# One queue for the first block's two pieces, and the sample's output products behind block 1, whose last half is accumulated in two banks

## The chip, the cores and the metric

The kernel runs on one core of a Trainium2 chip. The metric is the device time of one execution in microseconds (us), and the profile is one execution taken by the hardware profiler. The engines are named as in the profile: PE is TensorE's products, PEld its weight loads, ACT is ScalarE, DVE is VectorE, POOL is GpSimd, SP is SyncE; a q behind a name is the engine's own instruction stream (DMA issues, semaphores).

## The reference

One step of a hybrid encoder layer for two groups that share all weights: a prompt of 256 frames and a sample of 32 frames of a running stream, 288 rows in all, width 1024. One input projection feeds an mLSTM branch (4 heads of 256) and a sparse attention branch (8 heads of 128); both are gated, projected and summed to `mixed`. What the change touches is the end of it, and the mLSTM state that the prompt leaves:

```python
C_new = decay * C + einsum('bhs,bshk,bshv->bhkv', w_s, k, v)
n_new = decay * n + einsum('bhs,bshk->bhk', w_s, k)
...
mixed = sigmoid(ga) * (branch_a @ w_out_a) + sigmoid(gb) * (branch_b @ w_out_b)
return layer_norm(DN_ALPHA * x + mixed @ w_o, ln_g, ln_b)
```

The outputs are y for prompt and sample, K, V and indexer keys, and the state C, n and m of both groups.

## The kernel before

The weights are cut into tiles of 1024 x 128, in the order of `tile_order`. Every tile is loaded by SyncE (`load_tile`), split into a high part by ScalarE (`split_hi`, line 130) and a low part by VectorE (`split_lo`, line 137), and multiplied on TensorE three times per 128 rows: high by high, high by low, low by high (`product`). All instructions of an engine run in the order in which the program issues them; the order is written out by hand: the loop of lines 1080 to 1092 goes over the tiles, and `at(slot, fn)` hangs further steps on a tile, which `side()` issues in the middle of that tile's products, in the order in which they were hung there.

**The start.** The first five tiles are loaded in eight blocks of 128 rows, with the matching rows of x (`lead`). Block 0 comes in two pieces: x and the first tile (416 columns), issued by SyncE (line 162), and the other four tiles (512 columns), issued by ScalarE on its own queue (line 163). Blocks 1 to 7 follow on SyncE's queue (line 165). ScalarE casts x to xh (line 170) and the weights to their high part (line 177). Until the first piece is there, TensorE runs 18 products on zeros (`keep_warm`).

**The output weights.** The last eight tiles, `wo`, are 128 rows of w_o each. `natural(t, rows)` multiplies them with `mixed` as the stationary side: rows 0 and 1 are the prompt's two blocks of 128 frames, each in two PSUM banks of 512 columns (yn, line 941); rows 2 is the sample, 32 frames x 1024 columns laid out as 4 groups of 32 partitions x 256 columns, 64 products from the raw weights (line 945). For the first four wo tiles both blocks are multiplied tile by tile; between block 0 and block 1 `side()` issues `k_weighted(h)` for head h (four transposes of its keys into a bank kt, line 687; two halves scaled into kwh by ScalarE, line 691, and the remainder into kwl by VectorE, line 692), and in the fourth tile also `state_prompt(0)`: two times six products of head 0's state (lines 704 to 706), each copied out by ScalarE (line 707), and the output's DMA, issued by ScalarE (line 711). For the last four tiles (`late`) `finish()` goes column half by column half instead: block 0, the sample, block 1; then the states of heads 1 to 3.

**The layer norm.** VectorE forms alpha * x + y in z (`residual`, line 1000), takes bn_stats of each half (line 1002), aggregates them and adds eps (lines 989, 990), GpSimd raises that to -1/2 (line 991), VectorE subtracts the mean and multiplies by g (`centred`, line 1006), and scales and adds b by halves (`scaled`, line 1011), behind which SyncE writes each half of 512 columns (line 1015). The sample goes through the same in 128 x 256 form (lines 1027 to 1042); its statistics are gathered from four groups of 32 partitions and spread back by small copies (lines 1030, 1033, 1035). VectorE's order is: block 0, the sample's statistics, block 0's scaling, first half of block 1, the sample's last two steps, second half of block 1, block 1's scaling.

PSUM has eight banks in two pools: six of `bank()` (tag side), two of tag proj, which the tiles' products and the state products use in turn. Before, kt is of the six.

## Time and profile before

| | us |
|---|---|
| median of 3 runs | 433.31 (433.23 to 433.58) |
| the profiled execution, its own time | 433.03 |
| its span in the profile | 431.3 |
| PE busy, share of the span | 424.0, 98% |
| PEld busy | 412.8, 96% |
| DVE busy | 300.3, 70% |
| ACT busy | 232.5, 54% |
| POOL busy | 23.0, 5% |
| granted TensorE clock, mean | 0.999 |

The span is what the profile shows between the first and the last instruction; the run's own time holds a little before and behind it. Busy shares are averages over stages with different limits. Times within the profile are counted from the span's start. A wait is given in brackets behind the instruction that waited, with what released it.

### The profile page before, as it was taken

How to read it: one execution, taken by the hardware profiler on the slowest of the kernel's cores; microseconds unless marked ns; L12 is line 12 of the kernel's file. 1: busy time of each engine (PE TensorE's matmuls, PEld its weight loads, DVE VectorE, ACT ScalarE, POOL GpSimd, SP SyncE). 2: the span in 40 equal slices, each digit the busy share in tenths (PEclk: the TensorE clock that was granted, in tenths of full speed). 3: DMA queues.
4: the chain of work that ended last, by engine and by line, in shares of the span. 5: the costliest groups of instructions: out<-in, count | busy, mean ns of one | idle time of the engine just before them, and what ended most of it. 6: DMA issues, size and time to landing. Idle time of an engine off the chain costs nothing.

```text
span 431.3 us, 8450 instructions
## 1 busy us (share of the span) xinstructions
PE 424.0 (98%) x3320; PEld 412.8 (96%) x3320; DVE 300.3 (70%) x607; ACT 232.5 (54%) x466; POOL 23.0 (5%) x46
## 2 busy tenths in 40 slices
PE   8999999999999999999999999999999999999994
PEld 7999999999999999999999999999999999998874
DVE  5779888898656665666999887776544465565674
ACT  6776556464475665667695464555343444445402
POOL 2000000021000000000001101101000000000031
PEclk9999999999999999999999999999999999999999
DMA  8996969757845544745554456444665567543014
GB/s 305 337 347 189 280 199 326 240 188 204 293 163 141 154 133 120 256 128 147 147 147 147 106 167 218 134 146 134 181 177 159 158 183 256 155 141 122 26 48 137
DMA packets 23471, 78.05 MB, mean 181 GB/s; under 512 B 2804, under 2 KB 5572, under 8 KB 22632
## 3 DMA queue, kind: packets, MB, share of 16 engines
q1 hardware_dynamic: 22568, 76.21, 57.0%
q10 hardware_dynamic: 864, 1.32, 0.9%
q8 instruction: 26, 0.43, 0.4%
q14 instruction: 13, 0.11, 0.1%
HBM read 71.77 MB, written 7.64 MB: 184 GB/s over the span
## 4 chain that ended last, share of the span: by engine, by line
PE 96%; DVE 1%; DMA 1%; ACT 1%; POOLq 0%; DVEq 0%; issue 0%
PE pj L923 26%; PE pj L922 26%; PE pj L924 25%; PE yn L941 5%; PE pj L960 3%; DMA wst_k<-in_first 1%; PE yn L945 1%; PE apt L592 1%; ACT wh L130 0%; PE al L573 0%; PE ix L416 0%; PE ix L417 0%; PE s L633 0%; PE av L602 0%; PE vt L646 0%; PE kt L687 0%
## 5 line engine op out<-in xcount | busy, mean ns | idle before, releaser
L922 PE MATMUL pj<-xh,wh 128*128 128x288 f32 x704 | 209.8, 298 | 0.1
L923 PE MATMUL pj<-xl,wh 128*128 128x288 f32 x704 | 207.7, 295 | 0.0
L924 PE MATMUL pj<-xh,wl 128*128 128x288 f32 x704 | 207.5, 295 | 0.0
L130 ACT CAST wh<-wst 128x1024 fp32r<-128x1024 f32 x112 | 117.8, 1052 | 128.9 <-PE pj L923 78.1
L137 DVE TENSOR_TENSOR wl<-wst,wh 128x1024 fp32r<-128x1024 f32 x112 | 136.2, 1219 | 29.0 <-ACT wh L130 28.7
L922 PEld LDWEIGHTS pj<-xh,wh 128*128 128x128 f32 x704 | 132.4, 188 | 1.0 <-issue 0.4
L923 PEld LDWEIGHTS pj<-xl,wh 128*128 128x128 f32 x704 | 132.4, 188 | 0.1
L924 PEld LDWEIGHTS pj<-xh,wl 128*128 128x128 f32 x704 | 132.3, 188 | 0.0
L922 PE MATMUL pj<-bbh,wh 128*128 128x288 f32 x64 | 19.1, 298 | 0.0
L923 PE MATMUL pj<-bbl,wh 128*128 128x288 f32 x64 | 19.0, 296 | 0.0
L923 PE MATMUL pj<-bal,wh 128*128 128x288 f32 x64 | 18.9, 295 | 0.0
L924 PE MATMUL pj<-bah,wl 128*128 128x288 f32 x64 | 18.9, 295 | 0.0
L924 PE MATMUL pj<-bbh,wl 128*128 128x288 f32 x64 | 18.8, 294 | 0.0
L922 PE MATMUL pj<-bah,wh 128*128 128x288 f32 x64 | 18.8, 293 | 0.0
L941 PE MATMUL yn<-wh,mxh 128*128 128x512 f32 x32 | 13.0, 407 | 0.0
L941 PE MATMUL yn<-wl,mxh 128*128 128x512 f32 x32 | 12.7, 396 | 0.1
L941 PE MATMUL yn<-wh,mxl 128*128 128x512 f32 x32 | 12.6, 394 | 0.0
L922 PEld LDWEIGHTS pj<-bbh,wh 128*128 128x128 f32 x64 | 12.1, 188 | 0.0
L924 PEld LDWEIGHTS pj<-bbh,wl 128*128 128x128 f32 x64 | 12.0, 188 | 0.0
L922 PEld LDWEIGHTS pj<-bah,wh 128*128 128x128 f32 x64 | 12.0, 188 | 0.0
L923 PEld LDWEIGHTS pj<-bal,wh 128*128 128x128 f32 x64 | 12.0, 188 | 0.0
L924 PEld LDWEIGHTS pj<-bah,wl 128*128 128x128 f32 x64 | 12.0, 188 | 0.0
(494 smaller groups left out, 576.7 us busy)
## 6 DMA issues: line engine op xcount, KB each, us to landing
wst<-in_w SPq DMA_DIRECT2D x112, 512.0 KB, 3.7
wst_k<-in_first SPq DMA_DIRECT2D x7, 464.0 KB, 5.9
rscr<-rrow SPq DMA_DIRECT2D x2, 768.0 KB
out_k<-kbT SPq DMA_DIRECT2D x1, 1152.0 KB
stC<-in_state_C SPq DMA_DIRECT2D x1, 1028.0 KB
out_C_sample<-stC SPq DMA_DIRECT2D x1, 1028.0 KB
bm<-rscr SPq DMA_DIRECT2D x1, 1024.0 KB
ckT<-in_cache_k SPq DMA_DIRECT2D x1, 1024.0 KB
```

The lines of the kernel that those rows point to most:

```text
L130: act.copy(split[t][0], stage[t])
L137: dve.tensor_tensor(wl, stage[t], wh.bitcast(F32), OP.subtract)
L592: pe.transpose(p[:, 128 * i:128 * i + 128], lg[:, c:c + 128], ident)
L922: pe.matmul(p[:, :T], lhsT=wh[:, c], rhs=h[:, k], start=(k == 0), stop=False)
L923: pe.matmul(p[:, :T], lhsT=wh[:, c], rhs=l[:, k], start=False, stop=False)
L924: pe.matmul(p[:, :T], lhsT=wl[:, c], rhs=h[:, k], start=False, stop=(k == KT - 1))
L941: pe.matmul(p, lhsT=x[:, k, r], rhs=w[:, c], start=first and i == 0, stop=last and i == 2)
L945: pe.matmul(p[32 * q:32 * q + 32, 0:256], lhsT=lazy["mxs"][:, k], rhs=stage[t][:, 256 * q:256 * q + 256], start=first, stop=last)
L960: pe.matmul(p[t][:, new], lhsT=w[:, 128 * t:128 * t + 128], rhs=x[:, k, new], start=(k == 0 and w is wh and x is xh), stop=(k == KT - 1 an ...
```

## The change

It does four things. (1) Block 0's second piece is issued by SyncE behind the first, not by ScalarE. (2) The bank kt is taken from the two of tag proj, and in the fourth wo tile `state_prompt(0)` is issued ahead of `k_weighted(3)`. (3) Block 1's second half is accumulated in two banks of 256 columns, in all eight wo tiles, and statistics are taken of 256 columns everywhere (four records per row instead of two). (4) In `finish()` the order is: block 0, block 1, sample, states, on TensorE; block 0, block 1 to its first scaled half, sample, with block 1's second scaled half between the sample's last two steps, on VectorE. Four small copies of the sample's mean go from GpSimd to VectorE.

```diff
     sp.dma_start(lead[0][:, 0:cut], a["first"][:, 0, 0:cut])
-    act.dma_start(lead[0][:, cut:LEAD], a["first"][:, 0, cut:])
+    sp.dma_start(lead[0][:, cut:LEAD], a["first"][:, 0, cut:])
...
-        p = bank(f"kt{h}")
+        p = ps.tile([128, 512], F32, name=f"kt{h}", tag="proj", bufs=2)
...
-    def natural(t, rows, columns=(0, 1)):
+    pieces = (((0, 512), (512, 1024)), ((0, 512), (512, 768), (768, 1024)))
+
+    def natural(t, rows, some=None):
...
-            lazy["yp", rows] = [bank(f"yn{rows}{c}") for c in range(2 if rows < 2 else 1)]
+            lazy["yp", rows] = [bank(f"yn{rows}{c}") for c in range(len(pieces[rows]) if rows < 2 else 1)]
...
-            for c in columns:
-                p = lazy["yp", rows][c]
-                c = slice(512 * c, 512 * c + 512)
+            for j, (c0, c1) in enumerate(pieces[rows]):
+                if some not in (None, j):
+                    continue
+                p = lazy["yp", rows][j][:, :c1 - c0]
+                c = slice(c0, c1)
...
-            dve.bn_stats(bst[:, b, c], z[:, b, half])
+            for c in range(c0, c1, 256):
+                dve.bn_stats(bst[:, b, c // 256], z[:, b, c:c + 256])
...
-        for rows in (0, 2, 1):
-            for c in range(2 if rows < 2 else 1):
-                for t in late if rows < 2 else range(POS["wo", 0], NT):
-                    natural(t, rows, (c,))
-        for c in range(2):
-            residual(0, c)
-        rs = centred(0)
+        for b in range(2):
+            for j in range(len(pieces[b])):
+                for t in late:
+                    natural(t, b, j)
+        for t in range(POS["wo", 0], NT):
+            natural(t, 2)
+        for j in range(len(pieces[0])):
+            residual(0, j)
+        rs = centred(0)
+        for c in range(2):
+            scaled(0, rs, c)
+        for j in range(len(pieces[1])):
+            residual(1, j)
+        rs = centred(1)
+        scaled(1, rs, 0)
...
-        for q in range(4):
-            pool.tensor_copy(nr[32 * q:32 * q + 32, 0:1], mv[r, 0:1])
         for q in range(3):
             pool.tensor_copy(nr[32 * q:32 * q + 32, 1:2], nr[r, 1:2])
-        scaled(0, rs)
-        for c in range(2):
-            put(0, c)
-        residual(1, 0)
+        for q in range(4):
+            dve.tensor_copy(nr[32 * q:32 * q + 32, 0:1], mv[r, 0:1])
         dve.scalar_tensor_tensor(zs, zs, nr[:, 0:1], lazy["gs"], op0=OP.subtract, op1=OP.mult)
+        scaled(1, rs, 1)
         dve.scalar_tensor_tensor(zs, zs, nr[:, 1:2], lazy["bs"], op0=OP.mult, op1=OP.add)
         sp.dma_start(ap_of(o["y"], TP * D, [[256, 4], [D, TS], [1, 256]]), zs)
-        residual(1, 1)
-        rs = centred(1)
-        state_prompt(1)
-        scaled(1, rs)
-        for c in range(2):
-            put(1, c)
-        for h in range(2, AH):
+        for h in range(1, AH):
             state_prompt(h)
...
+    at(POS["wo", 0] + 3, state_prompt, 0)
     for h in range(AH):
         at(POS["wo", 0] + h, k_weighted, h)
-    at(POS["wo", 0] + 3, state_prompt, 0)
```

`scaled(b, rs, c)` now does one half and issues its output.

ScalarE in the fourth wo tile and behind it, before. L130 is the high part of a weight tile (the first row that of the last tile but one, the last row that of the last tile), L691 the scaled keys of head 3, L707 and L711 the state of head 0:

```order
L130 CAST wh_5136<-wst_4938 128x1024
L691 ACTIVATE kwh<-kt_5146,gnat 128x256 x2
L707 COPY oc_all<-c_5156 128x257
L707 COPY oc_all<-c_5164 128x257
L711 DMA out_C_prompt<-oc_all 128x514
L130 CAST wh_5180<-wst_4971 128x1024
```

The same stretch of the change:

```order
L130 CAST wh_5146<-wst_4938 128x1024
L707 COPY oc_all<-c_5157 128x257
L707 COPY oc_all<-c_5165 128x257
L711 DMA out_C_prompt<-oc_all 128x514
L691 ACTIVATE kwh<-kt_5174,gnat 128x256 x2
L130 CAST wh_5193<-wst_4971 128x1024
```

Head 3's two activations, on which VectorE's kwl (line 692) and, in VectorE's order, the low parts of the last two tiles follow, now stand behind the two copies and the DMA issue of head 0's state.

VectorE from block 1's first residual to the end, before. z is the prompt's rows, sq the sample's, yn_5078 and yn_5079 are block 1's banks:

```order
L1000 SCALAR_TENSOR_TENSOR z__5055<-xn,yn_5078 128x512
L1002 BN_STATS bst<-z__5055 128x6
L1040 SCALAR_TENSOR_TENSOR sq<-sq,nr_5281 128x256
L1041 SCALAR_TENSOR_TENSOR sq<-sq,nr_5281 128x256
L1000 SCALAR_TENSOR_TENSOR z__5055<-xn,yn_5079 128x512
L1002 BN_STATS bst<-z__5055 128x6
L989 BN_AGGR mv_5303<-bst 128x2
L990 TENSOR_SCALAR mv_5303<-mv_5303 128x1
L1006 SCALAR_TENSOR_TENSOR z__5055<-z__5055,mv_5303,lngb 128x1024
L1011 SCALAR_TENSOR_TENSOR z__5055<-z__5055,nr_5304,lngb 128x512 x2
```

The end of it in the change, from block 1's last two steps on:

```order
L1012 SCALAR_TENSOR_TENSOR z__5055<-z__5055,mv_5313,lngb 128x1024
L1017 SCALAR_TENSOR_TENSOR z__5055<-z__5055,nr_5314,lngb 128x512
L1038 SCALAR_TENSOR_TENSOR sq<-sq,yn_5257 128x256
L1039 BN_STATS bss<-sq 128x6
L1041 COPY bss<-bss 32x6 x3
L993 BN_AGGR mv_5326<-bss 32x2
L994 TENSOR_SCALAR mv_5326<-mv_5326 32x1
L1046 COPY nr_5327<-mv_5326 32x1 x4
L1047 SCALAR_TENSOR_TENSOR sq<-sq,nr_5327 128x256
L1017 SCALAR_TENSOR_TENSOR z__5055<-z__5055,nr_5314,lngb 128x512
L1049 SCALAR_TENSOR_TENSOR sq<-sq,nr_5327 128x256
```

The whole of the sample's part now stands behind block 1's first scaling, where before it was spread over the steps of both blocks; its last step is VectorE's last.

## Rows read from the trace of the kernel before

**Rows 1.** The page, chain of work that ended last, share of the span by engine.

```profile
PE 96%; DVE 1%; DMA 1%; ACT 1%; POOLq 0%; DVEq 0%; issue 0%
```

**Rows 2.** Timeline of the start: start us, us, engine line op out<-in, [idle before <-releaser].

```profile
0.80 0.41 ACTq L163 DMA_DIRECT2D wst_k<-in_first  x1
...
1.13 3.48 PE L148 MATMUL warm_p<-warm 128*128 128x256 bf16 x18 [1.13 <-DVE warm L143]
...
4.53 0.43 ACT L170 CAST xh<-wst_k 128x288 fp32r<-128x288 f32 x1 [2.00 <-DMA wst_k<-in_first]
...
6.09 0.72 ACT L177 CAST wh_k<-wst_k 128x640 fp32r<-128x640 f32 x1
...
7.27 0.75 PE L960 MATMUL pj<-xh,wh_k 128*128 128x288 f32 x5
```

**Rows 3.** DMA queues, window 2.8 to 3.4: packets, MB, share of 16 engines (q10: ScalarE's).

```profile
q10 hardware_dynamic: 47, 0.10, 49.9%
```

**Rows 4.** Timeline of the fourth wo tile and the late tiles, 402 to 409.

```profile
402.66 0.60 PE L687 MATMUL kt<-cst,kaT 128*128 128x128 f32 x4
...
403.29 0.47 ACT L691 ACTIVATE kwh<-kt,gnat 128x256 fp32r<-128x256 f32 x1 [0.74 <-PE kt L687]
...
404.69 0.64 ACT L707 COPY oc_all<-c 128x257 f32<-128x257 f32 x2
...
404.83 0.48 DVE L692 SCALAR_TENSOR_TENSOR kwl<-kt,gnat,kwh 128x256 fp32r<-128x256 f32 x1 [0.54 <-ACT kwh L691]
...
405.23 1.22 DVE L137 TENSOR_TENSOR wl<-wst,wh 128x1024 fp32r<-128x1024 f32 x1
405.36 0.35 ACTq L711 DMA_DIRECT2D out_C_prompt<-oc_all  x1
...
406.12 1.05 ACT L130 CAST wh<-wst 128x1024 fp32r<-128x1024 f32 x1 [0.78 <-PE yn L941]
...
407.20 1.22 DVE L137 TENSOR_TENSOR wl<-wst,wh 128x1024 fp32r<-128x1024 f32 x1 [0.75 <-ACT wh L130]
...
408.47 0.19 PEld L941 LDWEIGHTS yn<-wl,mxh 128*128 128x128 f32 x1 [0.51 <-DVE wl L137]
```

**Rows 5.** Chain that ended last, from 405 us: start us, us, what.

```profile
411.99 3.59 PE yn L945 x64
415.58 5.80 PE yn L941 x24
```

**Rows 6.** Windows, PE alone, 36 state products: stretch, us, busy (x), clock, DMA share, GB/s.

```profile
421.20:425.48 4.28, 4.28 (x36) 1.00 0.27 92
```

**Rows 7.** Timeline of the layer norm, 412 to 427.

```profile
412.02 0.69 DVE L1000 SCALAR_TENSOR_TENSOR z__5055<-xn,yn 128x512 f32<-128x512 f32 x1 [1.30 <-PE yn L941]
412.75 0.69 DVE L1002 BATCH_NORM_STATS2 bst<-z__5055 128x6 f32<-128x512 f32 x1
...
415.65 0.42 DVE L1027 SCALAR_TENSOR_TENSOR sq<-sq,yn 128x256 f32<-128x256 f32 x1 [0.58 <-PE yn L945]
...
416.10 0.43 DVE L1028 BATCH_NORM_STATS2 bss<-sq 128x6 f32<-128x256 f32 x1
...
416.56 0.52 DVE L1030 COPY bss<-bss 32x6 f32<-32x6 f32 x3
...
417.70 1.06 POOL L991 TENSOR_TENSOR nr<-mv,mhalf 32x1 f32<-32x1 f32 x1 [2.23 <-DVE mv L990]
...
423.09 0.15 DVE L990 TENSOR_SCALAR mv<-mv 128x1 f32<-128x1 f32 x1
...
424.89 1.42 DVE L1011 SCALAR_TENSOR_TENSOR z__5055<-z__5055,nr,lngb 128x512 f32<-128x512 f32 x2 [0.45 <-POOL nr L991]
```

**Rows 8.** Timeline of SyncE's queue: the issue of the sample's output.

```profile
421.32 0.59 SPq L1042 DMA_DIRECT2D out_y<-sq  x1
```

**Rows 9.** DMA queue of SyncE in the windows 424 to 424.5 and 429 to 430.

```profile
q1 hardware_dynamic: 26, 0.02, 13.1%
...
q1 hardware_dynamic: 26, 0.04, 11.1%
```

More of the change, by code (lines that the diff above doesn't have):

```diff
@@ L968, in load_tail @@
         lazy["zs"], lazy["gs"], lazy["bs"], lazy["xs"] = (sq[:, i] for i in range(4))
-        lazy["bst"] = sb("bst", [128, 2, 2, 6], tag="sg", bufs=3)
+        lazy["bst"] = sb("bst", [128, 2, 4, 6], tag="sg", bufs=3)
         lazy["bss"] = sb("bss", [128, 4, 6])
@@ L996, in finish, with residual @@
         g, be = lazy["g"], lazy["b"]
-        def residual(b, c):
-            half = slice(512 * c, 512 * c + 512)
-            dve.scalar_tensor_tensor(z[:, b, half], lazy["xn"][:, b, half], ALPHA, lazy["yp", b][c],
+        def residual(b, j):
+            c0, c1 = pieces[b][j]
+            part = slice(c0, c1)
+            dve.scalar_tensor_tensor(z[:, b, part], lazy["xn"][:, b, part], ALPHA, lazy["yp", b][j][:, :c1 - c0],
                                      op0=OP.mult, op1=OP.add)
-            dve.bn_stats(bst[:, b, c], z[:, b, half])
+            for c in range(c0, c1, 256):
+                dve.bn_stats(bst[:, b, c // 256], z[:, b, c:c + 256])
         def centred(b):
@@ L1007, in centred, with scaled @@
             return nr[:, 1:2]
-        def scaled(b, rs):
-            for c in (slice(0, 512), slice(512, 1024)):
-                dve.scalar_tensor_tensor(z[:, b, c], z[:, b, c], rs, be[:, c], op0=OP.mult, op1=OP.add)
-        def put(b, c):
+        def scaled(b, rs, c):
             c = slice(512 * c, 512 * c + 512)
+            dve.scalar_tensor_tensor(z[:, b, c], z[:, b, c], rs, be[:, c], op0=OP.mult, op1=OP.add)
             sp.dma_start(o["y"][128 * b:128 * b + 128, c], z[:, b, c])
         late = range(NT - 4, NT)
-        for rows in (0, 2, 1):
-            for c in range(2 if rows < 2 else 1):
-                for t in late if rows < 2 else range(POS["wo", 0], NT):
-                    natural(t, rows, (c,))
-        for c in range(2):
-            residual(0, c)
-        rs = centred(0)
+        for b in range(2):
[7 more added lines that the diff above has]
+        rs = centred(0)
+        for c in range(2):
+            scaled(0, rs, c)
[3 more added lines that the diff above has]
+        scaled(1, rs, 0)
         p, = lazy["yp", 2]
```

## The prediction

> **What bounds the kernel now.** I read the chain that ended last first: 96% of it is TensorE [rows 1], so time taken off TensorE's stream, or put on it, moves the end one for one until the last stage. The change touches three places, each of which has its own limit, so I read each from the timeline.
>
> At the start the first cast (xh, ScalarE) begins at 4.53, because piece 1 of block 0 lands then; TensorE passes the time with 18 warm-up products until 1.13 + 3.48 = 4.61 [rows 2]. While piece 1 is on its way, the second queue, which carries piece 2 alone, holds 49.9% of the 16 engines' time [rows 3].
>
> In the stage of the output weights, from 391 us, TensorE never waits but once: at 408.47 a weight load has sat idle 0.51, released by the low part (wl) of the last tile, which VectorE began at 407.20, as soon as ScalarE's cast of 406.12 was done [rows 4].
>
> Behind the products VectorE is the limit. From its first step on the second half of block 0, at 412.02, to the end of the last scaling, 424.89 + 1.42 = 426.31, are 14.29 us, and of these it waits only 0.58 for the sample's products and 0.45 for GpSimd's power [rows 7]. TensorE's last state product is not what ends the kernel. From 426.31 to the span's end at 431.3 are 5.0 us of transfer and closing.
>
> The sum below is made against the profiled execution, 433.03 us, which lies 0.28 below the median of the three runs, 433.31.
>
> **1. The start.** Piece 2 is issued behind piece 1 on SyncE's queue instead of beside it: it, and the seven loads behind it, are issued one issue later, 0.41 [rows 2]. Piece 1 no longer shares the engines with it. The gain has a ceiling. TensorE could start at 4.61 at best. Block 1's weights are cast by 6.09 + 0.72 = 6.81 and TensorE takes them up at 7.27 [rows 2], so from 0.46 on, block 1 (whose bytes arrive behind the same total as before) would be late instead. Below, the bound is a loss of 0.41: piece 1 no earlier, everything behind it an issue later. I take a gain of **0.35**, near the ceiling, because half of the engines' time before the landing goes to the other piece. The warm-up products cover what is earlier than 4.61.
>
> On the same place a rule of the Trainium skill speaks against the change: DMA: Bandwidth & Descriptors, section Issuing engines are not separate DMA queues, says that transfers from several engines run on the same 16 DMA engines and interleave, and that issuing from several only saves issue time. The trace agrees with the interleaving (both queues are busy together); taken alone the rule would make the one queue a loss of the saved issue, and the sum 0.76 higher.
>
> **2. Head 3's keys behind head 0's state.** The banks kt move to the two buffers that the state products use, and kt3 now follows the 12 state products of head 0 on TensorE. On TensorE this costs next to nothing: 36 such products take 4.28, 0.119 each [rows 6], and the bank that kt3 needs is copied out while the second six run. On ScalarE and VectorE it costs. Before, kt3's transposes begin at 402.66 and ScalarE's kwh at 403.29; the two casts and two subtractions alternate, so that the last kwl begins at 404.83 and wl of the last tile but one at 405.23 [rows 4]. Now:
> - state products from 402.66, the last begins at 403.97 and ends 0.28 later, 404.25; ScalarE's second copy follows it and is done 0.4 later, at 404.65 (two take 0.64 in a row [rows 4]);
> - the state's DMA issue, 0.35 [rows 4], now stands ahead of kwh on ScalarE: kwh at 405.06, 1.77 later than before;
> - kwh, kwl, kwh, kwl as before, so wl of the last tile but one begins at 405.23 + 1.77 = 407.00 and ends at 408.22; the cast of the last tile, 1.05, ends at 407.54 and waits for nobody; wl of the last tile follows on VectorE and ends at 409.40.
>
> TensorE would take up these two lows at 407.58 and, after the first stall, at 409.1. It gets them at 408.27 and 409.45. The first product of block 0's second half then starts at 410.01 instead of 409.04: **+0.97**. In between nobody else is delayed; behind it, everything is, since VectorE's chain starts from these products. Bounds: nothing, if kwh begins by 404.4, and 1.3.
>
> **3. Block 1's last half in two banks.** 48 products of 256 columns take the place of 24 of 512. The nearest row is 0.119 for 258 columns [rows 6], against 0.24 for 512 (24 in 5.80 [rows 5]): **0**, with up to +0.1.
>
> **4. VectorE behind the products.** The sample's steps go behind block 1's, between the two halves of its last scaling. I count from the step that stood at 412.02, with starts of neighbours as spacing [rows 7]:
> - block 0: residual 0.73, two statistics of 256 in 0.90 (one: 0.43; one of 512: 0.69), aggregate 0.29 (from the sample's, below), to the small step at 1.92; from there to the scaling 1.80 as in block 1 (423.09 to 424.89); both scalings 1.34: 5.06.
> - block 1: residual 0.71, statistics 0.82, two residuals and statistics of 256 in 0.45 + 0.37 + 0.45 + 0.46, aggregate 0.29: 8.61; 1.80 and the first scaling 0.67: 11.08.
> - sample: residual 0.45, statistics 0.46, three copies, aggregate and small step 0.56 + 0.29 + 0.18 = 1.03 (416.56 to the power at 417.70, less the hand-over), four copies that GpSimd did before 0.74 (three took 0.52): 13.76; centring 0.51, block 1's second scaling 0.70 (half of 1.42), last step 0.48 (both a little over the 0.42 that 256 columns take with the residual): **15.45**.
>
> GpSimd's power for the sample (1.06) and its three copies lie beside this from 13.1 and end at about 14.9, just ahead of the last step. The sample's products, 3.59 [rows 5], now end at about 9.5 and are wanted at 11.08, so that wait is gone (0.58); but block 0's power, which the sample's steps covered, now stands bare as block 1's does (0.45). Against 14.29 this is **+1.16** (bounds +0.6, if neighbours overlap as some do, and +1.6).
>
> **5. The last transfer.** Before, the kernel ends behind two transfers of 256 KB; now behind the sample's 128 KB. Before, that transfer is issued at 421.32 [rows 8] and its queue is still moving bytes, at 13.1%, after 424.0, some 3.0 us from issue [rows 9], though it is the smaller transfer. Before, the last bytes flow until 429.5 (11.1% in the window from 429 [rows 9]), and 1.8 pass to the span's end. So 3.0 + 1.8 = 4.8 behind the last step, against 5.0: **-0.2** (bounds -1.7, if it ran at the blocks' rate, and +0.3).
>
> Sum: -0.35 + 0.97 + 0 + 1.16 - 0.2 = +1.58. Against the profiled execution this is 434.6, against the median **434.9 us**.
>
> **The rivals.**
> - *Not slower: the split is not late.* If kwh of head 3 begins by 404.4 (ScalarE free of the state's copy and issue by then), both lows are in time and the 0.97 fall away: 433.9, within 0.2% of before. For it: VectorE stood idle 0.75 in that stretch [rows 4]. Against: on ScalarE the two copies and the issue stand ahead of kwh, and ScalarE works in order.
> - *The start loses.* Piece 1 lands as before, the issue is paid: +0.76, 435.6. For it: no row shows SyncE's queue moving faster when it is alone. Against: [rows 3].
> - *The sample's transfer is quick at the end.* Its slowness is neighbours' doing and goes; up to 1.5 less: 433.4. Against: 2.7 behind its issue it was still moving [rows 9].
> - *The narrow products wait for their weights.* If none starts sooner than a load's 0.19 [rows 4], the 24 in TensorE's stream ahead of block 0's end cost 24 x 0.07 = 1.7: 436.6. Against: 258 columns went at 0.119 with the same loads [rows 6].
>
> **How the numbers follow.** Two per mille, 0.87 us, is what a measurement of this kernel can tell from no change. Forecast 0.60, by itself 434.2 to 435.7; split not late 0.16; start loses 0.10; quick transfer 0.07; narrow products 0.03; something that makes it faster, unseen here, 0.04. Slower by over 0.2% (over 434.18): the forecast but for its edge (0.58), the lost start, the narrow products and a fifth of the split rival, 0.74. Same 0.20, faster 0.06. The range 433.4 to 435.7 leaves out the narrow products and the faster side.
>
> **What would show it.** Right: the first xh cast before 4.2 and block 1's products some 0.35 earlier; weight loads of the late tiles twice idle on wl, 0.7 and 0.4; the step of 412.02 at about 412.6; VectorE's last step at 428.1, the sample's output issued after it, and a span of 432.9. Wrong: a single short wait on wl; a last step before 427; or the last bytes less than 2.5 behind the sample's issue.

## The result, and the profile after

The changed kernel takes **435.73 us** in the median of 4 runs (435.34 to 436.14), the kernel before 433.31 (433.23 to 433.58): ratio 1.0056, 95% interval 1.0041 to 1.0071. It is slower, as forecast, but by 2.42 us where 1.58 was forecast, and 435.73 lies just outside the range (433.4 to 435.7). The profiled execution, the shortest of the four, took 435.34 with a span of 433.3, against 433.03 and 431.3 before.

The page's chain of the changed kernel, share of the span by engine, answers to [rows 1]: TensorE gave up two per cent, VectorE took them.

```profile
PE 94%; DVE 3%; POOL 1%; ACT 1%; issue 0%; POOLq 0%; ACTq 0%
```

Timeline of its start (start us, us, engine line op out<-in, [idle before <-releaser]), as [rows 2]:

```profile
1.12 4.02 PE L148 MATMUL warm_p<-warm 128*128 128x256 bf16 x18 [1.12 <-DVE warm L143]
...
1.26 0.42 SPq L163 DMA_DIRECT2D wst_k<-in_first  x1
...
1.72 3.85 SPq L165 DMA_DIRECT2D wst_k<-in_first  x7
...
3.29 0.43 ACT L170 CAST xh<-wst_k 128x288 fp32r<-128x288 f32 x1 [1.21 <-DMA wst_k<-in_first]
...
4.80 0.59 PE L964 MATMUL pj<-xh,wh_k 128*128 128x288 f32 x1
...
5.67 1.03 PE L964 MATMUL pj<-xh,wh_k 128*128 128x224 f32 x4
...
6.70 0.43 ACT L170 CAST xh<-wst_k 128x288 fp32r<-128x288 f32 x1 [2.02 <-DMA wst_k<-in_first]
7.04 0.72 ACT L177 CAST wh_k<-wst_k 128x640 fp32r<-128x640 f32 x1
...
7.82 0.84 PE L964 MATMUL pj<-xh,wh_k 128*128 128x288 f32 x5
```

Piece 1 lands 1.24 earlier (3.29 for 4.53). But ScalarE then waits 2.02 for block 1, its cast of block 1's weights stands at 7.04 for 6.09 before, and TensorE's products of block 1 begin at 7.82 for 7.27. The start has lost 0.55 where a gain of 0.35 was forecast; from the wo stage on it is 0.65 (its first yn product in the chain is at 392.42, for 391.77). TensorE shows no wait there, because block 0's products ran at half pace (four of 224 columns in 1.03; at full pace 0.59 to 0.61) and filled the time.

So two things hold block 1's products back in this trace at once. Its weights are cast only at 7.04 + 0.72 = 7.76 (6.81 before), and the trace's first entry of the granted clock, 1.00, the higher of its two levels, stands at 7.16 (3.91 before), where the pace of the products doubles; for the time ahead of that entry the views show 1.00 too, so only the pace tells. The second needs no edit: in e17 below, whose start is that of before, this entry stands at 7.06, and the wo stage begins at 392.33, 0.56 later than before. The 0.65 of this one trace can therefore not be put down to block 1's landing alone; the runs below tell the two apart.

The stage of the late tiles, as [rows 4]:

```profile
405.39 0.39 ACTq L711 DMA_DIRECT2D out_C_prompt<-oc_all  x1
...
405.82 0.47 ACT L691 ACTIVATE kwh<-kt,gnat 128x256 fp32r<-128x256 f32 x1 [0.46 <-PE kt L687]
...
407.22 1.04 ACT L130 CAST wh<-wst 128x1024 fp32r<-128x1024 f32 x1
...
407.36 0.48 DVE L692 SCALAR_TENSOR_TENSOR kwl<-kt,gnat,kwh 128x256 fp32r<-128x256 f32 x1 [0.54 <-ACT kwh L691]
...
407.76 2.35 DVE L137 TENSOR_TENSOR wl<-wst,wh 128x1024 fp32r<-128x1024 f32 x2
...
409.02 0.19 PEld L945 LDWEIGHTS yn<-wl,mxh 128*128 128x128 f32 x1 [1.05 <-DVE wl L137]
...
410.16 0.19 PEld L945 LDWEIGHTS yn<-wl,mxh 128*128 128x128 f32 x1 [0.61 <-DVE wl L137]
```

Head 3's kwh stands behind the state's DMA issue (405.39 + 0.39; the transposes kt, which its bracket names, were done before), and the two lows of the late tiles follow each other on VectorE, 407.76 to 410.11. A weight load waits for each, where one waited before. Block 0's second half starts at 410.74 for 409.04; less the 0.65 of the start this stage cost 1.05.

VectorE and GpSimd behind the products, as [rows 7], and SyncE's last issue, as [rows 8]:

```profile
413.73 0.69 DVE L1005 SCALAR_TENSOR_TENSOR z__5055<-xn,yn 128x512 f32<-128x512 f32 x1 [1.24 <-PE yn L945]
...
423.82 0.75 DVE L1017 SCALAR_TENSOR_TENSOR z__5055<-z__5055,nr,lngb 128x512 f32<-128x512 f32 x1 [0.45 <-POOL nr L995]
...
426.43 0.63 DVE L1046 COPY nr<-mv 32x1 f32<-32x1 f32 x4
...
426.54 0.55 POOL L995 TENSOR_TENSOR nr<-mv,mhalf 32x1 f32<-32x1 f32 x1 [2.75 <-DVE mv L994]
...
427.15 1.35 POOL L1044 COPY nr<-nr 32x1 f32<-32x1 f32 x3
...
428.54 0.48 DVE L1049 SCALAR_TENSOR_TENSOR sq<-sq,nr 128x256 f32<-128x256 f32 x1 [0.30 <-POOL nr L1044]
...
429.05 0.57 SPq L1050 DMA_DIRECT2D out_y<-sq  x1
```

From 413.73 to 429.02 are 15.29 us, 1.00 more than the 14.29 of before. From VectorE's last step to the span's end (433.3) are 4.28, 0.71 to 0.74 less than before (spans are given to 0.1). SyncE's queue, in the window 431 to 432, as [rows 9]:

```profile
q1 hardware_dynamic: 90, 0.09, 26.4%
```

The sample's 128 KB go out at 0.09 MB a microsecond with a quarter of the engines' time. The Trainium skill, DMA: Bandwidth & Descriptors, section Why a DMA increments its semaphore by 16 and not by 1, says that a transfer uses the largest number of engines, up to 16, that divides the slowest dimension (other than 1) of both its sides. Here that dimension is 4 in the output and 128 in SBUF, which would be 4 of 16 engines; the 26.4% agree with it.

One part is in no view. A run's time less its span is 1.73 in the profiled run before, and 2.00 to 2.05 in the four runs after: 0.31 more in the profiled one.

### The profile page after: what moved, and what is told of

The parts are those of the page before. It is cut to its first block, busy times and chain, and to the rows that moved or that the text cites. A ratio compares the mean times of both kernels' runs of the same rounds, so it can differ in the third digit from the quotient of the medians.

```text
span 433.3 us, 8503 instructions
## 1 busy us (share of the span) xinstructions
PE 425.5 (98%) x3344; PEld 415.4 (96%) x3344; DVE 301.4 (70%) x616; ACT 232.8 (54%) x466; POOL 22.5 (5%) x42
## 3 DMA queue, kind: packets, MB, share of 16 engines
q10 hardware_dynamic: 720, 1.05, 0.7%
## 4 chain that ended last, share of the span: by engine, by line
PE 94%; DVE 3%; POOL 1%; ACT 1%; issue 0%; POOLq 0%; ACTq 0%
PE pj L923 26%; PE pj L922 25%; PE pj L924 25%; PE pj L964 3%; PE yn L945 3%; PE warm_p L148 1%; POOL nr L995 1%; PE apt L592 1%; DVE bst L1008 1%; DVE wl L137 1%; DVE z__5055 L1017 0%; PE al L573 0%; DVE z__5055 L1005 0%; PE ix L417 0%; PE ix L416 0%; PE s L633 0%
## 5 line engine op out<-in xcount | busy, mean ns | idle before, releaser
L130 ACT CAST wh<-wst 128x1024 fp32r<-128x1024 f32 x112 | 117.8, 1052 | 127.3 <-PE pj L923 82.2
L945 PE MATMUL yn<-wl,mxh 128*128 128x512 f32 (+1 forms) x40 | 14.1, 354 | 0.8 <-DVE wl L137 0.8
L945 PE MATMUL yn<-wh,mxh 128*128 128x512 f32 (+1 forms) x40 | 14.3, 357 | 0.0
L945 PE MATMUL yn<-wh,mxl 128*128 128x512 f32 (+1 forms) x40 | 14.0, 349 | 0.0
L707 ACT COPY oc_all<-c 128x257 f32<-128x257 f32 x8 | 3.0, 374 | 18.8 <-PE c L706 18.8
```

The source lines that it names most:

```text
L130: act.copy(split[t][0], stage[t])
L707: act.copy(oc[:, kd], p[:, :257])
L945: pe.matmul(p, lhsT=x[:, k, r], rhs=w[:, c], start=first and i == 0, stop=last and i == 2)
```

## The experiments

Each kernel was timed in 5 rounds against the kernel before on the same chip. That kernel's median was 432.89 for e1 to e4, 433.01 for e5 to e8, 433.02 for e9 to e12, 433.08 for e13 and e14, 433.14 for e15 and e16, 433.09 for e17. A figure with a sign (+1.32) is a kernel's median less that; the change's own is +2.42. "Block 1's cast" is ScalarE's first cast of block 1, at 5.76 before and 6.70 in the change. The 95% interval of the change's ratio is +1.8 to +3.1 in microseconds.

### One part undone

**e1**, the change with piece 2 back on ScalarE's queue:

```diff
-    sp.dma_start(lead[0][:, cut:LEAD], a["first"][:, 0, cut:])
+    act.dma_start(lead[0][:, cut:LEAD], a["first"][:, 0, cut:])
```

> The changed kernel with block 0's second piece back on ScalarE's queue; all else as changed. Theory Q (the one queue holds block 1 back: it is issued 0.45 later and lands 0.9 later, and TensorE has no work until its weights are cast): block 1's first cast again at about 5.8 instead of 6.70, TensorE's product on the first output tile 0.65 earlier, so 435.1 us. Rival C (TensorE's clock rose late, at 7.16 instead of 3.91, and that is chance or comes from the earlier first product): with chance the median stays near 435.7, and runs with the lower mean clock are the longer ones.

434.76 us (434.47 to 435.32), ratio 1.0040 [1.0027, 1.0053]: +1.87, 0.55 less than the change. But the intervals overlap (+1.2 to +2.3 here), so the time alone doesn't show it. The profile is of the longest run, 435.32. Block 1's cast is back at 6.16, yet its products begin no earlier than in the change:

```profile
7.92 0.74 PE L964 MATMUL pj<-xh,wh_k 128*128 128x288 f32 x5
```

Block 0 landed late in it (first cast at 4.88) and the higher clock came at 6.66. So this run doesn't rule out rival C, the late clock.

**e2**, the kernel before with that line alone:

```diff
-    act.dma_start(lead[0][:, cut:LEAD], a["first"][:, 0, cut:])
+    sp.dma_start(lead[0][:, cut:LEAD], a["first"][:, 0, cut:])
```

> The kernel before with only the two pieces on one queue. Theory Q: +0.65, 433.95 us, in every run, whatever its mean clock. Rival C: runs with mean clock 0.999 take 433.3 as before, runs with 0.996 or so are 0.6 or more longer. The prediction's step (gain 0.35): 432.95.

434.21 us in 12 runs (433.30 to 436.56), ratio 1.0032 [1.0022, 1.0043], so +1.32 (+0.9 to +1.9): twelve runs in which the one line costs time. Rival C's sign doesn't come: the shortest run, 433.30, has a mean clock of 0.996, and 434.62 has 0.999. But that sign could not tell: e15's profiled run has a mean of 1.000, although its higher clock came only at 10.33. The profile is of its longest run, 436.56; two rows of its timeline, and two of its windows (stretch, us, PE busy (x), clock, DMA share, GB/s):

```profile
8.07 0.43 ACT L170 CAST xh<-wst_k 128x288 fp32r<-128x288 f32 x1 [3.39 <-DMA wst_k<-in_first]
...
9.18 0.84 PE L960 MATMUL pj<-xh,wh_k 128*128 128x288 f32 x5 [2.84 <-ACT wh_k L177]
```

```profile
10.00:12.00 2.00, 2.00 (x15) 0.66 1.03 414
12.00:14.00 2.00, 2.00 (x11) 0.50 1.03 400
```

The higher clock came early here (3.81), so the wait is bare: block 1 came 2.3 later than before, TensorE stood for 2.84, and behind the wait, from 10.64 to 14.05, the granted clock was 0.50, the lower of its two levels. The same edit costs from 0.4 to 3.7 us from run to run; in this one the wait was paid twice.

**e3**, the change with k_weighted and state_prompt in the old order and kt in the old banks:

```diff
-        p = ps.tile([128, 512], F32, name=f"kt{h}", tag="proj", bufs=2)
+        p = bank(f"kt{h}")
...
-    at(POS["wo", 0] + 3, state_prompt, 0)
     for h in range(AH):
         at(POS["wo", 0] + h, k_weighted, h)
+    at(POS["wo", 0] + 3, state_prompt, 0)
```

> The changed kernel with kt taken from the six banks again and head 3's keys ahead of head 0's state. Theory: TensorE's two waits for the low parts of the last two tiles (together 1.3 us with their slow restarts) become the one short one of before; first product of block 0's second half 1.05 earlier, all behind it too: 434.7 us. Rival (VectorE's chain has slack behind it, or the six banks no longer suffice and the sample's bank waits for kt3): no change, 435.7.

436.08 us (434.68 to 437.11), ratio 1.0068 [1.0050, 1.0087]: +3.19, not below the change. The six runs fall in two groups, 434.68 to 435.28 and 436.88 to 437.11. In the profiled one (434.87) the wait on wl is one of 0.5 again and VectorE's step is at 413.33, 0.40 earlier than in the change although the wo stage begins 0.59 later. So the stage gave back 1.0, and the start, with block 1's products at 8.41 behind a wait of 0.81, took part of it. The three longer runs have a mean clock of 0.993 for 0.997 to 0.998 in the others, as a fall like e2's would leave it; none of them was traced. As a time it was inconclusive; e17 repeats the question on the old start.

**e4**, the change with the order of before at the end (sample's products and steps between the blocks), the narrow banks kept:

```diff
-        for b in range(2):
+        for b in (0, None, 1):
+            if b is None:
+                for t in range(POS["wo", 0], NT):
+                    natural(t, 2)
+                continue
             for j in range(len(pieces[b])):
...
```

> The changed kernel with the order of before at the end, on TensorE (block 0, sample, block 1, states) and on VectorE (the sample's steps between those of the blocks, the mean's copies on GpSimd), but block 1's last half still in two banks of 256. Theory: the order costs 1.0 on VectorE (15.3 us from the second half of block 0 to its last step against 14.3) and gives back 0.74 in the last transfers, so undoing it gains little: 435.3 to 435.6. Because the narrow last piece then shortens the chain behind TensorE's last product by up to 0.5, as low as 434.9. Rival (the order is most of the loss): 434.5 or less. Rival (the order gains): 436 or more.

435.10 us (434.77 to 435.52), ratio 1.0049 [1.0037, 1.0061]: +2.21. VectorE's steps take 14.45 from block 0's second residual, for 15.29; but block 1's products began at 8.30, 0.48 later than in the change, so the difference of the times understates the end. e5 has the end on the old start. This trace, with the change's start and the higher clock from 4.52, shows the cost of the late block 1 with the clock out of the way:

```profile
8.30 0.84 PE L964 MATMUL pj<-xh,wh_k 128*128 128x288 f32 x5 [1.66 <-ACT wh_k L177]
```

### One part alone

**e5**, the kernel before with the change's end (all of its diff from `natural` on, nothing at the start or in k_weighted).

> The kernel before with the change's end alone (the narrow banks, the sample's products behind block 1 and its steps last); the start and k_weighted are as before. Theory (the three parts add up): the end costs +1.00 in VectorE's chain, -0.74 between the sample's issue and the end of the span, +0.31 outside the span, so before + 0.57, about 433.5; from block 0's first residual to VectorE's last step 15.3 us, 4.25 us from the sample's issue to the end of the span, 2.05 us outside the span. Rival one (the end alone is free, and the 1.87 that the change without its start kept over before is all k_weighted): before within 0.2. Rival two (the end is most of that 1.87): before + 1.2 or more.

433.74 us (433.41 to 434.27), ratio 1.0016 [1.0007, 1.0024]: +0.73. Its last step and last issue:

```profile
426.69 0.49 DVE L1049 SCALAR_TENSOR_TENSOR sq<-sq,nr 128x256 f32<-128x256 f32 x1 [0.30 <-POOL nr L1044]
...
427.21 0.57 SPq L1050 DMA_DIRECT2D out_y<-sq  x1
```

15.30 from 411.88 to 427.18, 4.2 from there to the span's end (431.4), 2.0 outside the span: the three terms come back, and the theory stands. The 0.31 outside the span goes with which transfer is last: it is 2.0 to 2.1 in the change, e1, e3, e5 and e16, and 1.7 to 1.8 in the kernels that end with a block's rows.

**e6**, the narrow banks alone, in the order of before.

> The kernel before with the last half of block 1 in two banks of 256 columns and statistics by 256 columns, in the order of the kernel before; nothing else. Theory (narrow banks cost nothing and give nothing in this order, since VectorE still has the sample's two scalings ahead of block 1's last pieces): before within 0.3, 14.3 to 14.5 us from block 0's first residual to the last step. Rival (the narrow products wait for weights, twelve products of 256 columns more): before + 0.8 or more, TensorE's wo products end later by as much. Rival two (the shorter last piece shortens what stands behind the last product): before - 0.4 or less.

432.86 us (432.74 to 433.24), ratio 0.9996 [0.9987, 1.0005]. The narrow banks cost nothing and give nothing here; VectorE takes 14.45.

**e17**, k_weighted's part alone (e3's diff the other way round, on the kernel before).

> The kernel before with k_weighted's part alone: kt in the two buffers of the projections, head 0's state products ahead of head 3's keys; start and end as before. Theory (the split of the late tiles comes late, as predicted): TensorE's weight loads wait for wl twice, 1.6 to 1.7 us in all in place of 0.5, the step of 412.02 about 1.0 later, before + 0.9 to + 1.1, about 434.1. Rival (the wait is covered later, by VectorE's own slack or the transfers at the end): before within 0.3.

434.13 us (433.68 to 434.55), ratio 1.0021 [1.0012, 1.0030]: +1.04. Its two waits:

```profile
408.86 0.19 PEld L941 LDWEIGHTS yn<-wl,mxh 128*128 128x128 f32 x1 [1.03 <-DVE wl L137]
...
410.00 0.19 PEld L941 LDWEIGHTS yn<-wl,mxh 128*128 128x128 f32 x1 [0.60 <-DVE wl L137]
```

Its start is that of before and its block 1 is on time (cast at 5.62), yet its wo stage begins 0.56 later than before: the warm-up took 4.02 for 3.48 and block 0's first four products of 224 columns 1.03, at half pace (higher clock from 7.06). From its chain:

```profile
1.12 4.02 PE warm_p L148 x18
...
392.33 1.39 PE yn L941 x6
```

Less these 0.56, VectorE's step of 412.02 stands 0.97 later than before (413.55). Shown, then: the late split costs about 1.0 (0.97 in the trace, 1.04 in the medians), and nothing behind it takes any of that back.

### Why block 1 is late

**e8**, the kernel before with its 48-byte load of small ahead of block 1's load, so that blocks 1 to 7 are issued as late as in the change, on the two queues of before:

```diff
+    small = sb("small", [4, 3])
+    sp.dma_start(small, a["small"])
     for k in range(1, KT):
         sp.dma_start(lead[k][:, 0:LEAD], a["first"][:, k])
```

> The kernel before with its tiny load small (48 bytes, 0.37 us of issue) moved ahead of block 1's load, so that blocks 1 to 7 are issued as late as in the change (block 1 at 1.7 us) while the two pieces of block 0 stay on two queues. Theory O (in the change the one queue carries block 0's two pieces ahead of block 1's, and its packets go slowly after 3.4 us; the later issue itself is a small part): block 1's cast begins at 5.8 to 6.2 us, TensorE's block 1 products at 7.3 to 7.6, time before + 0 to 0.3. Theory D (the later issue of the seven loads is the cause): block 1's cast at 6.7 or later, products at 7.8 or later, time before + 0.6 or more, like the start of the change alone (+1.3).

436.33 us (435.92 to 436.92), ratio 1.0077 [1.0064, 1.0089]. By the time theory D (the later issue of the seven loads is the cause) would have won; the profile says no. Block 1's cast is at 6.07 and the first products end within 0.2 of before (19.79 for 19.59 in the chain); the other 3 us come up evenly all through the kernel. **e12** moves the tile alone and leaves the load where it was:

```diff
+    small = sb("small", [4, 3])
     for k in range(1, KT):
         sp.dma_start(lead[k][:, 0:LEAD], a["first"][:, k])
...
-    small = sb("small", [4, 3])
     sp.dma_start(small, a["small"])
```

> The kernel before with the tile small (12 bytes a partition) allocated ahead of the split weights' buffers, its load where it was: no instruction moves, the buffers wh and wl lie a few bytes further on in SBUF. In e8 all products of the projections ran at 300 and 297 ns in place of 298 and 295, from end to end. Theory (that is the tile's place, not the load's): the same 300 and 297 ns and before + 2.9 to + 3.3. Rival (the place of the tile means nothing, e8's extra came from its start): before within 0.3.

436.21 us (436.06 to 436.44), ratio 1.0072 [1.0060, 1.0085]. The costliest group of its page, and the same group of the kernel before, which the changed kernel's page shows with the same figures (out<-in, xcount | busy us, mean ns | idle):

```profile
L922 PE MATMUL pj<-xh,wh 128*128 128x288 f32 x704 | 211.1, 300 | 0.1
```

```profile
L922 PE MATMUL pj<-xh,wh 128*128 128x288 f32 x704 | 209.8, 298 | 0.1
```

So e8's extra is the place of a 12-byte tile, not the start. **e9** asks e8's question with a load whose tile lies where it lay:

```diff
+    sp.dma_start(sel, a["sel"])
     for k in range(1, KT):
...
-    sp.dma_start(sel, a["sel"])
```

> The kernel before with the load of sel (8 KB, into a tile that lies where it lay) moved ahead of block 1's load: blocks 1 to 7 are issued about 0.4 us later, as in the change, block 0's two pieces stay on two queues, and no tile moves in SBUF. Theory O (the one queue is what costs): block 1's cast at 5.8 to 6.3 us, the first products end within 0.3 of the kernel before, time before + 0 to 0.3. Theory D (the later issue of the seven loads costs): cast at 6.7 or later, before + 0.6 or more.

433.38 us (432.80 to 433.61), ratio 1.0004 [0.9995, 1.0013]. Block 1's cast at 5.65; block 2's waits 1.10. The later issue costs 0.36, which cannot be told from nothing (interval -0.2 to +0.6): theory D, which wanted 0.6 or more and a cast at 6.7, falls.

**e10**, block 0's pieces on SyncE's queue as in the change, block 1's load on ScalarE's:

```diff
-    act.dma_start(lead[0][:, cut:LEAD], a["first"][:, 0, cut:])
-    for k in range(1, KT):
+    sp.dma_start(lead[0][:, cut:LEAD], a["first"][:, 0, cut:])
+    act.dma_start(lead[1][:, 0:LEAD], a["first"][:, 1])
+    for k in range(2, KT):
         sp.dma_start(lead[k][:, 0:LEAD], a["first"][:, k])
```

> The kernel before with block 0's second piece on SP's queue and block 1's load on ACT's queue ahead of ScalarE's first cast: two queues again, SP with block 0 and blocks 2 to 7, ACT with block 1 alone. Theory O (blocks behind block 0 on its own queue land late; a block on the other queue doesn't): block 1's cast at 5.9 or earlier, before - 0.3 to + 0.2, unless block 2 is then the late one. Rival (any order with block 0's pieces on one queue makes the engines' packets slow after 3.4 us): block 1's cast at 6.5 or later, before + 0.6 or more.

433.82 us (433.63 to 435.04), ratio 1.0021 [1.0012, 1.0030]. The time is the rival's, the cause is neither's: block 1 is there when ScalarE gets to it, and now block 0 is late.

```profile
5.28 0.43 ACT L171 CAST xh<-wst_k 128x288 fp32r<-128x288 f32 x1 [2.76 <-DMA wst_k<-in_first]
```

The core moved 413 GB/s from 4 to 5 us, as before; from 3 to 4 us ScalarE's queue, with block 1, had 63.6% of the engines' time and SyncE's, with block 0, 34.0%, so the engines gave block 1 what block 0 needed.

**e11**, block 0 in one load on SyncE's queue:

```diff
-    sp.dma_start(lead[0][:, 0:cut], a["first"][:, 0, 0:cut])
-    act.dma_start(lead[0][:, cut:LEAD], a["first"][:, 0, cut:])
+    sp.dma_start(lead[0][:, 0:LEAD], a["first"][:, 0])
```

> The kernel before with block 0 in one load of 464 KB on SP's queue in place of two pieces: one queue, all packets of one size. Theory O (one queue): block 0's cast at about 4.1 to 4.8, block 1 late as in the change's start (cast 6.5 or later), before + 0.6 to + 1.3. Rival (the two sizes of packet in one queue are what goes badly): block 1's cast at 6.0 or earlier and before within 0.3.

433.30 us (432.80 to 433.73), ratio 1.0004 [0.9996, 1.0013]. Casts at 4.53 and 5.80, as before. One queue is not the cause, so theory O (the one queue is what costs) falls as it was put.

**e13**, block 0 in two loads on that queue, by partitions (all rows of 3,712 bytes):

```diff
-    sp.dma_start(lead[0][:, 0:cut], a["first"][:, 0, 0:cut])
-    act.dma_start(lead[0][:, cut:LEAD], a["first"][:, 0, cut:])
+    for c in (slice(0, 64), slice(64, 128)):
+        sp.dma_start(lead[0][c, 0:LEAD], a["first"][c, 0])
```

> The kernel before with block 0 in two loads on SP's queue again, as in the change, but cut by partitions (0 to 63, 64 to 127) and not by columns, so that every row of every load has one length, 3,712 bytes. Theory M (rows of two shorter lengths ahead of block 1's on one queue are what goes badly): as e11, block 1's cast at 6.1 or earlier, before within 0.4. Rival N (any second load ahead of block 1's on its queue does it): block 1's cast at 6.5 or later, before + 0.6 or more.

436.66 us (436.39 to 437.32), ratio 1.0090 [1.0076, 1.0103]. As a time it answers nothing: with two loads to wait for, ScalarE's table load moved behind the wait.

```profile
5.24 1.28 ACT L170 ACT_TABLE_LOAD   x1 [5.24 <-DMA wst_k<-in_first]
```

**e15** cuts that first cast in two, so that the table load stands at 0.80 again:

```diff
-        act.copy(xh[:, k], raw[:, 0:T])
+        for c in (slice(0, 64), slice(64, 128)) if k == 0 else (slice(0, 128),):
+            act.copy(xh[c, k], raw[c, 0:T])
```

> e13 with ScalarE's first cast in two of 64 partitions, each behind its own load (the table load then stands ahead of both, one cast of about 0.4 us is added). Theory N (a second load ahead of block 1's on its queue makes a slow stretch, whatever its rows): the core moves 300 GB/s or less from 4 to 5 us as in e13 (208), block 1's cast at 6.5 or later, before + 0.6 to + 1.5. Rival M (short rows): 400 GB/s from 4 to 5 us, block 1's cast at 6.2 or earlier, before + 0 to 0.4.

434.85 us (433.94 to 435.55), ratio 1.0036 [1.0024, 1.0048]: +1.71, block 1's cast at 6.63. The time holds more than the loads: in the profiled run, its longest, the higher clock came only at 10.33. What speaks to the question is what the core's DMA engines moved from 4 to 5 us, here in before, the change, e11 and e15:

```profile
DMA packets 125, 0.41 MB, mean 414 GB/s; under 512 B 13, under 2 KB 13, under 8 KB 125
```

```profile
DMA packets 94, 0.33 MB, mean 327 GB/s; under 512 B 6, under 2 KB 6, under 8 KB 94
```

```profile
DMA packets 122, 0.41 MB, mean 408 GB/s; under 512 B 12, under 2 KB 12, under 8 KB 122
```

```profile
DMA packets 68, 0.21 MB, mean 212 GB/s; under 512 B 11, under 2 KB 11, under 8 KB 68
```

Theory N stands by these rows: a second load of block 0 ahead of block 1's on the same queue makes a slow stretch, whatever the length of its rows; one load of all its bytes doesn't, nor does the small load of e9 (390 GB/s from 4 to 5 us), nor two pieces with block 1 on the other queue (e10). In the change the stretch had begun from 3 to 4 us (255 GB/s, for 364 before).

The rate is not all of it. By 6 us the change had received 1.24 MB for 1.39 before: 0.15 MB less, at 0.41 MB a microsecond about 0.35 us, while block 1 was 0.94 later. The rest is order: when block 1's cast began, 1.53 MB had come in (by 6.70) where before it was 1.31 MB (by 5.76); blocks 0 and 1 are 0.95 MB of it, and what is over belongs to later blocks. Why the packets go slowly there, and why more of the later blocks comes in ahead of block 1's last bytes, stays open.

**e16** puts e11's single load into the change.

> The change with block 0 in one load on SP's queue, in place of two on it; k_weighted and the end as in the change. Theory (the start's loss is the second load on the queue): block 1's cast at 5.8 to 6.1 us, 0.7 to 1.0 less than the change, about 434.8, as e1 (two queues). Rival (the loss is that of one queue, and e11 was luck): within 0.3 of the change, 435.5 or more.

434.64 us (434.46 to 435.07), ratio 1.0038 [1.0025, 1.0051]: +1.50 (+1.1 to +2.2), 0.92 less than the change. Block 1's cast at 5.61, its products at 7.15, and the core moved 419 GB/s from 4 to 5 us: the single load mends the start. How much of the 0.92 it is worth is less sure, since in this profile the higher clock came at 3.86 and in the change's at 7.16.

### The opposite order at the end

**e7**, the kernel before with the narrow banks, the sample's products ahead of both blocks and its steps ahead of block 1's:

```diff
-        for rows in (0, 2, 1):
...
+        for b in (None, 0, 1):
+            if b is None:
+                for t in range(POS["wo", 0], NT):
+                    natural(t, 2)
+                continue
```

> Start and k_weighted as before, narrow banks as in the change, and the sample's products ahead of both blocks', with the sample's VectorE steps ahead of block 1's: the opposite end of the order. Theory (what counts behind the last product is VectorE's chain and where the kernel's last transfer comes from): the steps behind the last product are those of 256 columns alone, 0.42 + 0.43 + 0.21 + 0.15 + 1.28 + about 0.4 + 1.42 = 4.3 us in place of 4.9, and the last transfer is a block's, 1.73 us outside the span: before - 0.6 to - 0.9, about 432.1. Rival (VectorE is the bound all through the end, whatever the order): its 14.3 us stand, before within 0.2.

432.50 us (432.12 to 433.50), ratio 0.9990 [0.9981, 0.9999]: the fastest of all, by 0.1%, at the edge of what can be told. The expected way there was wrong. VectorE works through to 426.96, later than before (426.31): from block 0's first residual (412.66) its steps take 14.30 us. What went is the wait on wl, which the sample's 64 products now cover. Weight loads on wl from 390 us, before (0.5 of idle behind VectorE) shown in [rows 4], here:

```profile
L945 PEld LDWEIGHTS yn<-wl,mxh 128*128 128x128 f32 x40 | 7.5, 188 | 0.9
```

TensorE's products end 0.34 earlier (0.10 of it from the start), the last state's output is issued at 425.94 for 426.27, and block 1's rows have the engines more to themselves: 3.8 us from VectorE's last step to the span's end, for 5.0.

**e14**, e7's order with the banks and statistics of the kernel before:

```diff
-        for rows in (0, 2, 1):
+        for rows in (2, 0, 1):
...
```

> The order of e7 with the two banks of 512 columns and the statistics of the kernel before: in e7 VectorE worked without a gap from 412.66 to 426.96, and block 1's last half in two pieces takes it 1.66 us (4 steps) in place of 1.37 (2 steps), statistics by 256 columns 0.75 in place of 0.69 three times. Theory (VectorE's chain bounds the end): 0.3 to 0.5 shorter than e7, before - 0.8 to - 1.0. Rival (the transfers of the states and of block 1 bound the end, VectorE's 0.4 is hidden): as e7, before - 0.4 to - 0.6. Rival two (in this order the narrow banks carry e7's gain): before within 0.2.

432.91 us (432.42 to 433.07), ratio 0.9994 [0.9985, 1.0002]. VectorE's chain from the sample's first step is 0.48 shorter than in e7 (16.77 for 17.25), and the time isn't: the first theory falls. The profile agrees once its start is taken off: its wo stage begins 0.59 later than e7's (higher clock from 6.54, for 5.06) and its span is 0.57 longer. Its interval and e7's overlap, so whether the narrow banks give e7 something stays open.

## Why the prediction was wrong, and where it was right

- **1, the start: wrong, and this is the step that failed.** Forecast -0.35; the edit alone cost +1.32 (e2), and the profile of the change has +0.65. The reasons taken from [rows 2, 3] held: piece 1 came early, even more than enough. What failed is the clause that block 1's "bytes arrive behind the same total as before", from which the ceiling of the gain and the bound of 0.41 on the loss were worked out. They arrived behind a larger total (1.53 MB for 1.31) and at a lower rate (327 GB/s for 414 from 4 to 5 us), and block 1's weights were cast by 7.76 in place of 6.81. With the clock early that is a bare wait on TensorE: 1.66 in e4, 2.84 in e2. In the change's own profile the late clock hides the wait and would by itself have cost about as much (0.56 in e17); the working has no term for it and takes "4.61 at best" from a run whose clock came early. One load in place of two mended the landing (e11, e16). The rival of the lost start (+0.76) had nearly the right price by luck: it let piece 1 land as before and charged the issue, and the issue alone is worth 0.56 at most (e9). The Trainium skill's sentence on issuing engines (DMA: Bandwidth & Descriptors, Issuing engines are not separate DMA queues) says that issuing from several saves only the time of issuing. By it one queue should cost no more than that: e11, one queue and one issue, agrees, with 0.28 that can't be told from nothing; e2, with +1.32, doesn't.
- **2, the late split: right.** Forecast +0.97, measured 1.05 in the profile and 1.04 alone (e17), through the queue of steps described: copies, issue, kwh, two lows in a row, two waits. The weight loads sat idle 1.05 and 0.61 where 0.7 and 0.4 were named as the sign, since a load's idle time counts from the end of the load before it. The rival that it would not be late falls.
- **3, the narrow banks: right**, 0 (e6).
- **4, VectorE behind the products: right in its working**, forecast +1.16, measured +1.00 (15.30 alone in e5). GpSimd's power on the sample took 0.55 where [rows 7] had 1.06, yet its copies ended last, not "just ahead of the last step": a wait of 0.30 remained.
- **5, the last transfer: mis-sized, and incomplete.** Forecast -0.2; in the span -0.74, outside it +0.31, so -0.43. The sample's output took as long as read from [rows 8, 9]; the 1.8 of closing behind the last bytes was the part that shrank, to about 1.3 behind bytes that ended at 432.0. Most of that only moved out of the span: from the last bytes to the end of the run's own time are 3.5 before and 3.3 after. That time outside the span belongs to the last transfer too was not considered.

Sum on the profiled runs: 0.65 + 1.05 + 1.00 - 0.74 + 0.31 = 2.27, against 435.34 - 433.03 = 2.31. Of the 0.69 by which this exceeds the forecast, the start is +1.00 and the split +0.08; the end took back 0.16 and the last transfer 0.23. That the median lies only just outside the range is luck to that extent: without these 0.39 it would be further out. The parts alone (1.32 + 1.04 + 0.73 = 3.09) come to more than the whole, 2.42, at the upper end of its interval (+3.1); the start is the part that differs most from run to run.

## What to carry to other kernels

A small first load that lands early is worth nothing if the load behind it comes late: check the landing of the second and third block before counting the first. And before a few tenths at the start of a profile are put down to an edit, compare the pace of the first products with that of a run whose start is untouched. Work that is put ahead of a cast or a copy on an engine that works in order is paid by whoever needs that cast, here two engines further on, and can be read off the timeline to a tenth of a microsecond. When a time moves and the waits don't, look at the mean of the costliest group: it may be the place of a tile.

## What was not expected of the hardware

- Two loads of block 0 ahead of block 1's on one queue: 208 to 327 GB/s from 4 to 5 us (the change, e2, e3, e4, e13, e15), where one load, or two on two queues, went at 408 to 419 (before, e1, e11, e16).
- The higher granted clock came between 3.76 and 7.06 us behind the same 18 warm-up products, in kernels whose start is that of before (before, e5, e6, e7, e14, e17); the latest began the wo stage 0.56 later than the kernel before.
- A tile of 12 bytes a partition allocated ahead of the split weights' buffers slows all projection products from 298 to 300 ns and the kernel by 3.2 us (e12), with no instruction moved.
- ScalarE's table load stood in front of its first cast's wait where that cast had one load to wait for (0.80 in e15), and behind it where it had two (5.24 in e13).
- The part of a run's time outside the span was 2.0 to 2.1 where the last transfer was the one that takes a quarter of the engines' time, and 1.7 to 1.8 where it was a block's.
